# Six of twelve row pairs by seven products in the second feed-forward product, on one core

## The chip, the cores and the metric

The kernel runs on one core of a Trainium2 chip. The metric is the device time of one execution in microseconds. Of the core's engines the text names PE (TensorE: matmuls, with its weight loads as PEld), DVE (VectorE), ACT (ScalarE), POOL (GpSimd) and SP (SyncE, which issues most transfers).

## The reference

A trunk of two layers over 256 tokens of 2048 features, in fp32. Each layer is a token mixer and a feed-forward part, each with a normalization in front and a residual sum behind:

```python
for layer in range(DEPTH):                      # 2
    hn = rms_norm(h, norm_mix[layer])
    mix = mlstm_mixer(hn, ...) if layer % 2 == 0 else rglru_mixer(hn, ...)
    h = h + mix
    h = h + swiglu(rms_norm(h, norm_ffn[layer]), ffn_w_in[layer], ffn_w_out[layer])
return rms_norm(h, norm_final)

def swiglu(x, w_in, w_out):                     # 2048 -> 2 x 5632 -> 2048
    g, u = jnp.split(x @ w_in, 2, axis=-1)
    return (jax.nn.silu(g) * u) @ w_out
```

The change concerns the product with `w_out` in both layers, and some memory that the first normalization and the first mixer use.

## The kernel before

**Numbers in two halves.** A fp32 matrix is split into a high half (a cast to fp32r on ACT, L452) and a low half (what is left, a subtraction on DVE, L453); `split_store` does both. A product is three matmuls: high by high (L390), high by low (L391), low by high (L392). For weights the halves are the tiles `whi` and `wlo`; the loaded weights are `raw`. Low halves come last, so the first matmul that reads a `wlo` (L391) is the one that waits if DVE is late.

**Pairs.** `paired` multiplies two blocks of 128 tokens with two blocks of 512 columns, over row blocks taken two at a time. A plain pair is 2 x 2 x 2 block products, 8 x 3 = 24 matmuls; DVE makes two `wlo` of 1024 columns for it. A pair in the list `seven` is multiplied by a scheme with seven products instead of eight, as Strassen's does: 21 matmuls, but DVE has to form four sums or differences of weight blocks (L403, L404, L405, L407, each 512 columns) and four splits (`s`, `u`, `v`, `t`, of 1024, 512, 1024 and 1024 columns; L401, L402, L406, L408). The third split, `v`, waits for L405. The seven products also need the activations in seven forms instead of four. `raw`, `whi` and `wlo` have six buffers each in the feed-forward layers (four in `wpool`, two in the layer's own pool); a seven-pair uses two of `raw` and four of each of the others, a plain pair two of each.

**A feed-forward layer** (`ffn`). The 5632 hidden columns are taken in two chunks, `CHUNKS`: of 6 and 5 groups of 512 columns. A group (`group`) is the first product for 512 columns of both halves: 8 row pairs, of which `SEVEN_IN` = 2, 4, 6 by seven; the first group of a layer takes the pairs in the order `FIRST`. Its result `e` is turned by `turn` into two row pairs of the hidden matrix, `hid`, with 7 or 4 forms a row pair, according to the list for the second product. This is put off by `later` and runs some steps into the next group. After the groups of a chunk come two calls of `add_out`, each the second product for 1024 of the 2048 output columns over the chunk's 12 or 10 row pairs, of which `SEVEN_OUT` says which go by seven. After the last seven-pair, `sums` and `mid` add the shared banks up and into `h` on DVE (L478 to L482, L778); after the last pair four more sums follow (L789). The very last product takes its pairs in another order, with the two last ones held back.

**Order.** The program is written in order; a scheduler fixes the order of each engine's queue ahead of time, and every engine works its queue in order. `later` and `run_pending` put small pieces of work between the steps of a product: `run_pending` is called once a step with the step's length, and starts the first piece that is due.

**The start.** `par_src` lists the small parameters. Seven transfers on SP bring them in as rows (`rows`, three tiles); `par_cols(i)` transposes one of the three sets on PE and copies it to `cols`. Set 0 holds the first gains and is needed at once. Sets 1 and 2 are transposed after the first product of the first mixer (`linear_wide` ... `"qk00"`, L516 to L518). Between the steps of that product the quarters 1 to 3 of the normalization `n0` are made, each followed by an empty piece:

```python
for q in range(1, 4):
    later(lambda q=q: n0.quarter(q))
    later(lambda: None)
```

`n0.quarter(3)` writes the tile with the tag `x3` of `xpool`. `mask` is a constant of the first mixer, made by POOL and read at L593. `const` is a pool that lives for the whole program; `mx` is the first mixer's and is freed after it.

Of the kernel before, what the change touches and what calls it, by code (L numbers as in the profile page):

```python
# [8 lines left out]
F32 = mybir.dt.float32  # L9
F32R = mybir.dt.float32r  # L10
AF = mybir.ActivationFunctionType
ALU = mybir.AluOpType
PSUM = bass.MemoryType.PSUM

P = 128
# [11 lines left out]
BIG = 1e30  # L27
AHEAD = 1000

SEVEN_IN = (2, 4, 6)  # L30
SEVEN_OUT = {12: (2, 4, 6, 8, 10), 10: (2, 4, 6, 8)}
FIRST = (0, 1, 3, 2, 5, 4, 6, 7)
SEVEN_VO = (3, 5)
CHUNKS = ((0, 6), (6, 11))
# [5 lines left out]
def kernel(  # L40
# [21 lines left out]
    nc = tc.nc  # L62
    const = ctx.enter_context(tc.tile_pool(name="const", bufs=1))
    small = ctx.enter_context(tc.tile_pool(name="small", bufs=2))
    wpool = ctx.enter_context(tc.tile_pool(name="wpool", bufs=4))
    xpool = ctx.enter_context(tc.tile_pool(name="xpool", bufs=1))
# [29 lines left out]
    def load_x():  # L96
        for q in range(4):
            nc.sync.dma_start(h[:, :, q * NB:(q + 1) * NB], xv[:, :, q * NB:(q + 1) * NB])
            if q < 2:
                for kg in (4 * q, 4 * q + 2):  # L100
                    if kg:
                        raw0[kg] = load_raw(m_w_in[0], 0, NB, kg)


    ident = const.tile([P, P], F32, name="ident")
# [7 lines left out]
    for i in range(12):  # L113
        nc.tensor.matmul(pwarm[:, 0:P], lhsT=ones, rhs=ones, start=(i == 0), stop=(i == 11))
    mhalf = const.tile([P, 2], F32, name="mhalf")
    nc.vector.memset(mhalf, -0.5)
    mask = const.tile([P, P], F32, name="mask")
    nc.gpsimd.memset(mask, 0.0)
    nc.gpsimd.affine_select(
        out=mask, in_=mask, compare_op=ALU.is_ge, fill=BIG, base=0,  # L120
        pattern=[[1, P]], channel_multiplier=-1,
    )


    par_src = [
        ("g_mix", norm_mix.rearrange("l (k p) -> (l k) p", p=P), 32),
# [5 lines left out]
        ("cw", r_conv_w.rearrange("l j (k p) -> (l j k) p", p=P), 64),  # L132
    ]
    par = {}
    rows = [const.tile([P, P], F32, name=f"rows{i}") for i in range(3)]
    cols = [const.tile([P, P], F32, name=f"cols{i}") for i in range(3)]
    part, at, used = 0, 0, [0, 0, 0]
    for name, src, n in par_src:
        if part == 0 and at or at + n > P:
            part, at = part + 1, 0  # L140
        nc.sync.dma_start(rows[part][at:at + n, :], src)
        if part == 0:
            load_x()
        par[name] = cols[part][:, at:at + n]
        at += n
        used[part] = at
# [3 lines left out]
    def par_cols(i):  # L150
        n = used[i]
        pt = misc(f"par{i}")
        nc.tensor.transpose(pt[:, 0:n], rows[i][0:n, :], ident[0:n, 0:n])
        with tc.high_priority(offset=AHEAD):
            return nc.vector.tensor_copy(cols[i][:, 0:n], pt[:, 0:n])

    gains = par_cols(0)


# [4 lines left out]
    def later(fn, after=0.0):  # L164
        pending.append((work[0] + after, fn))
# [60 lines left out]
    def linear_wide(w, c0, nk, act, act2, name, soon=2):  # L226

        ps = [acc(f"{name}_{f}") for f in range(4)]
        for k, hi, lo in stream(w, c0, nk):
            for f0 in (0, 2):  # L230
                for f in (f0, f0 + 1):
                    nc.tensor.matmul(ps[f], lhsT=hi[:, f * P:(f + 1) * P], rhs=act2(k), start=(k == 0), stop=False,  # L232
                                     skip_group_check=True)
                for f in (f0, f0 + 1):
                    nc.tensor.matmul(ps[f][:, 0:T], lhsT=lo[:, f * P:(f + 1) * P], rhs=act(k)[0], start=False,  # L235
                                     stop=(k == nk - 1), skip_group_check=True)
            run_pending(1.39, k >= soon)
        return ps
# [6 lines left out]
    def bc4(ap):  # L245
        return ap.unsqueeze(1).broadcast_to([P, 4, T])
# [226 lines left out]
    part = {}  # L473
# [19 lines left out]
    for i in range(6):  # L493
        nc.tensor.matmul(idle[:, 0:P], lhsT=ident, rhs=h[:, 0, 0:P], start=(i == 0), stop=(i == 5))
    for q in range(1, 4):
        later(lambda q=q: n0.quarter(q))
        later(lambda: None)
    n1 = Pairs("f0", par["g_ffn"][:, 0:16])

    def mlstm_mixer():  # L500
        with tc.tile_pool(name="mx", bufs=2) as mx:
            w = m_w_in[0]
            scratch["pool"] = mx
            ys = [[mx.tile([P, 4, T], F32R, tag=f"y{s}{j}", name=f"y{s}{j}", bufs=1) for s in "hl"] for j in range(4)]
            scratch["get"] = lambda: mx.tile([P, NT * 2 * (DV + 1)], F32, tag="vs", name="zt")[:, 0:4 * T]
            sel = mx.tile([H, H, P], F32R, tag="y", name="sel", bufs=1)
# [7 lines left out]
            gsel = mx.tile([4 * H, 2 * H], F32, name="gsel", bufs=1)  # L514
            nc.gpsimd.tensor_tensor(gsel, ident[0:4 * H, 0:2 * H], ident[0:4 * H, 2 * H:4 * H], op=ALU.add)
            ps_q0 = linear_wide(w, 0, NK, n0.act, n0.act2, "qk00", soon=0)  # L516
            par_cols(1)
            par_cols(2)  # L518
            with tc.issue_after(n0.last.ins):
                for q in range(4):  # L520
                    n0.stats(q)
# [115 lines left out]
            for half in range(2):  # L637
                for which, dst, sc in ((0, qT, 1.0), (1, kT, DK ** -0.5)):
                    ps = ps_q0
                    if half or which:  # L640
# [4 lines left out]
                        out=d4, in0=d4, scalar=sc, in1=bc4(n0.bc), op0=ALU.mult, op1=ALU.mult,  # L645
# [82 lines left out]
            project_out(m_w_out[0], NK, lambda k: (yh[k // 4][:, k % 4, :], yl[k // 4][:, k % 4, :]), n1)  # L728

    mlstm_mixer()  # L730


    def ffn(layer, n, nxt):
        with tc.tile_pool(name=f"ff{layer}", bufs=1) as fp:
# [56 lines left out]
            for c0, c1 in CHUNKS:  # L791
                np_ = 2 * (c1 - c0)
                seven = SEVEN_OUT[np_]
                hid = [
# [221 lines left out]
```

## Time and profile before

| | us |
|---|---|
| median of 3 runs | 2095.54 (2095.53 to 2095.84) |
| the profiled execution | 2092.44 |
| its span, first to last instruction | 2090.5 |
| PE busy | 2075.5 (99%) |
| PE weight loads busy | 1732.5 (83%) |
| DVE busy | 1838.1 (88%) |
| ACT busy | 1200.3 (57%) |
| granted clock of PE | 0.999 of full speed |

Times in the profile are from the start of the span. A row of the order of time has start, duration, engine, line, operation, output and inputs, the shape, the count, and in brackets the idle time of the engine before it with what ended it. A row of the waits has who waited for whom, microseconds in total, times, the longest. A row of the windows has the stretch, its length, and for PE, PEld, DVE, ACT and POOL the busy time with the number of instructions, then the granted clock, the share of the transfer engines and GB/s. The first layer's groups start at 394 us and its feed-forward part ends at about 1090; the second layer's goes from 1384 to the end.

### The profile page before, as it was taken

Reading aid. Unit: us, or ns where it says so; the run is one execution under the profiler, and the core shown is the slowest. Engines: PE = TensorE matmul, PEld = TensorE weight load, DVE = VectorE, ACT = ScalarE, POOL = GpSimd, SP = SyncE. Lnnn points to the kernel's source line nnn. Section 1 sums busy time; section 2 is a strip of 40 time slices with the busy share of each in tenths; the row PEclk is TensorE's granted clock in tenths of the full one; section 3 lists DMA queues with packets and bytes.
Section 4 is the critical chain, followed back from the end, with each engine's and each line's share of the span. In section 5 each row is a group of like instructions: output and inputs, shape, how many; then the busy total and the mean of one; then the engine's idle time right before and its main releaser. Section 6 shows DMA issues by size and latency. Waiting matters only on the chain.

```text
span 2090.5 us, 27102 instructions
## 1 busy us (share of the span) xinstructions
PE 2075.5 (99%) x9770; PEld 1732.5 (83%) x9770; DVE 1838.1 (88%) x2362; ACT 1200.3 (57%) x1553; POOL 26.1 (1%) x44
## 2 busy tenths in 40 slices
PE   9999999999999999999999999999999999999997
PEld 7888888888888888888888888888888888888886
DVE  7678886799999999999997888679999999999998
ACT  6446555565555555555656778556555555555554
POOL 0000000000000000000000000000000000000010
PEclk9999999999999999999999999999999999999999
DMA  7556655656565665665656666666655666656564
GB/s 217 172 171 190 182 181 177 204 188 228 173 200 202 201 201 201 202 218 185 202 186 177 191 183 191 191 192 208 206 193 185 201 207 202 205 198 220 191 202 141
DMA packets 211374, 405.71 MB, mean 194 GB/s; under 512 B 14552, under 2 KB 14760, under 8 KB 211112
## 3 DMA queue, kind: packets, MB, share of 16 engines
q1 hardware_dynamic: 210520, 401.89, 59.7%
q10 hardware_dynamic: 720, 2.10, 0.3%
q8 instruction: 76, 1.25, 0.2%
q14 instruction: 58, 0.48, 0.1%
HBM read 401.84 MB, written 2.10 MB: 193 GB/s over the span
## 4 chain that ended last, share of the span: by engine, by line
PE 94%; DVE 3%; issue 1%; ACT 1%; DMA 1%; POOL 0%; POOLq 0%; SPq 0%; ACTq 0%; DVEq 0%
PE p L392 15%; PE p L391 15%; PE p L390 15%; PE po L391 7%; PE po L392 7%; PE po L390 7%; PE rec L232 3%; PE gb L232 3%; PE po L208 3%; PE po L206 3%; PE po L207 3%; PE vo L390 2%; PE vo L392 2%; PE vo L391 2%; PE qk L232 2%; PE gb L235 1%
## 5 line engine op out<-in xcount | busy, mean ns | idle before, releaser
L452 ACT CAST whi<-raw 128x1024 fp32r<-128x1024 f32 (+1 forms) x812 | 768.3, 992 | 652.6 <-DVE raw L405 354.7
L453 DVE TENSOR_TENSOR wlo<-raw,whi 128x1024 fp32r<-128x1024 f32 (+1 forms) x812 | 897.4, 1149 | 94.8 <-ACT whi L452 90.5
L390 PE MATMUL p<-whi,z_f 128*128 128x512 f32 x1342 | 523.8, 390 | 0.0
L392 PE MATMUL p<-whi,z_f 128*128 128x512 f32 x1342 | 522.2, 389 | 0.0
L391 PE MATMUL p<-wlo,z_f 128*128 128x512 f32 x1342 | 522.2, 389 | 0.0
L392 PEld LDWEIGHTS p<-whi,z_f 128*128 128x128 f32 x1342 | 251.9, 188 | 52.3
L391 PEld LDWEIGHTS p<-wlo,z_f 128*128 128x128 f32 x1342 | 252.0, 188 | 51.6
L390 PEld LDWEIGHTS p<-whi,z_f 128*128 128x128 f32 x1342 | 252.0, 188 | 51.6
L178 DVE TENSOR_TENSOR wlo<-raw,whi 128x1024 fp32r<-128x1024 f32 (+1 forms) x161 | 195.2, 1215 | 87.7 <-ACT whi L176 87.5
L391 PE MATMUL po<-wlo,h 128*128 128x512 f32 x668 | 260.6, 390 | 1.7 <-DVE wlo L453 1.7
L392 PE MATMUL po<-whi,h 128*128 128x512 f32 x668 | 260.0, 389 | 0.0
L390 PE MATMUL po<-whi,h 128*128 128x512 f32 x668 | 259.3, 390 | 0.0
L176 ACT CAST whi<-raw 128x1024 fp32r<-128x1024 f32 (+1 forms) x161 | 168.0, 1046 | 130.7 <-PE po L208 58.7
L391 PEld LDWEIGHTS po<-wlo,h 128*128 128x128 f32 x668 | 125.4, 188 | 29.4 <-DVE wlo L453 3.5
L392 PEld LDWEIGHTS po<-whi,h 128*128 128x128 f32 x668 | 125.4, 188 | 25.9
L390 PEld LDWEIGHTS po<-whi,h 128*128 128x128 f32 x668 | 125.3, 188 | 25.9 <-ACT whi L452 0.2
L390 PE MATMUL vo<-whi,x_m 128*128 128x512 f32 x240 | 95.8, 399 | 0.5 <-DVE yl L697 0.5
L392 PE MATMUL vo<-whi,x_m 128*128 128x512 f32 x240 | 93.5, 390 | 0.0
L391 PE MATMUL vo<-wlo,x_m 128*128 128x512 f32 x240 | 93.5, 390 | 0.0
L232 PE MATMUL qk<-x_m,whi 128*128 128x512 f32 x256 | 81.1, 399 | 0.0
L232 PE MATMUL rec<-x_m,whi 128*128 128x512 f32 x256 | 80.6, 396 | 0.0
L232 PE MATMUL gb<-x_m,whi 128*128 128x512 f32 x256 | 80.4, 395 | 0.0
(272 smaller groups left out, 2431.6 us busy)
## 6 DMA issues: line engine op xcount, KB each, us to landing
raw<-in_ffn_w_in_dram SPq DMA_DIRECT2D x352, 512.0 KB, 4.9
raw<-in_ffn_w_out_dram SPq DMA_DIRECT2D x176, 512.0 KB, 5.4
raw<-in_m_w_in_dram SPq DMA_DIRECT2D x95, 512.0 KB, 4.0
raw<-in_r_w_in_dram SPq DMA_DIRECT2D x64, 512.0 KB, 3.9
raw<-in_m_w_out_dram SPq DMA_DIRECT2D x32, 512.0 KB, 3.9
raw<-in_r_w_out_dram SPq DMA_DIRECT2D x32, 512.0 KB, 3.9
gr<-in_r_gate_w_dram SPq DMA_DIRECT2D x8, 512.0 KB, 3.6
h<-in_x_dram SPq DMA_DIRECT2D x4, 512.0 KB, 8.2
```

Source lines behind the costliest of these rows:

```text
L176: cast = nc.scalar.copy(hi[:, at, 0:ncols], r)
L178: nc.vector.tensor_tensor(lo[:, at, 0:ncols], r, hi[:, at, 0:ncols].bitcast(F32), op=ALU.subtract)
L206: nc.tensor.matmul(o, lhsT=ah[:, bs], rhs=hi, start=(k == 0), stop=False)
L207: nc.tensor.matmul(o, lhsT=ah[:, bs], rhs=lo, start=False, stop=False)
L208: nc.tensor.matmul(o, lhsT=al[:, bs], rhs=hi, start=False, stop=(k == nk - 1))
L232: nc.tensor.matmul(ps[f], lhsT=hi[:, f * P:(f + 1) * P], rhs=act2(k), start=(k == 0), stop=False, skip_group_check=True)
L235: nc.tensor.matmul(ps[f][:, 0:T], lhsT=lo[:, f * P:(f + 1) * P], rhs=act(k)[0], start=False, stop=(k == nk - 1), skip_group_check=True)
L390: nc.tensor.matmul(o, lhsT=ah, rhs=bh, start=i not in begun, stop=False)
L391: nc.tensor.matmul(o, lhsT=ah, rhs=bl, start=False, stop=False)
L392: nc.tensor.matmul(o, lhsT=al, rhs=bh, start=False, stop=stop and p == end[i])
L452: nc.scalar.copy(dst_hi, src)
L453: nc.vector.tensor_tensor(dst_lo, src, dst_hi.bitcast(F32), op=ALU.subtract)
```

## The change

In `SEVEN_OUT` the 12-pair products get six pairs by seven instead of five, at other places, and the 10-pair products keep four, at other places. Neighbouring pairs (4 and 5, 7 and 8) are then both by seven. Row pairs 5 and 7 are stored in seven forms and row pair 6 in four, so one tile grows more than before. The rows of the parameters move from `const` into one tile with the tag `x3` of `xpool`, which quarter 3 of `n0` overwrites; for that, `par_cols(1)` and `par_cols(2)` move ahead of quarter 3, into the steps of the first product, in place of two empty pieces. `mask` moves from `const` to `mx` and is made there.

```diff
-SEVEN_OUT = {12: (2, 4, 6, 8, 10), 10: (2, 4, 6, 8)}
+SEVEN_OUT = {12: (2, 4, 5, 7, 8, 10), 10: (2, 4, 5, 8)}
...
-    mask = const.tile([P, P], F32, name="mask")
-    nc.gpsimd.memset(mask, 0.0)
-    nc.gpsimd.affine_select(
-        out=mask, in_=mask, compare_op=ALU.is_ge, fill=BIG, base=0,
-        pattern=[[1, P]], channel_multiplier=-1,
-    )
...
-    rows = [const.tile([P, P], F32, name=f"rows{i}") for i in range(3)]
+    rows = xpool.tile([P, 3, P], F32, tag="x3", name="rows")
...
-        nc.sync.dma_start(rows[part][at:at + n, :], src)
+        nc.sync.dma_start(rows[at:at + n, part, :], src)
...
-        nc.tensor.transpose(pt[:, 0:n], rows[i][0:n, :], ident[0:n, 0:n])
+        nc.tensor.transpose(pt[:, 0:n], rows[0:n, i, :], ident[0:n, 0:n])
...
     for q in range(1, 4):
+        if q == 3:
+            for i in (1, 2):
+                later(lambda i=i: par_cols(i))
         later(lambda q=q: n0.quarter(q))
-        later(lambda: None)
+        if q < 2:
+            later(lambda: None)
...
+            mask = mx.tile([P, P], F32, name="mask", bufs=1)
+            nc.gpsimd.memset(mask, 0.0)
+            nc.gpsimd.affine_select(
+                out=mask, in_=mask, compare_op=ALU.is_ge, fill=BIG, base=0,
+                pattern=[[1, P]], channel_multiplier=-1,
+            )
...
             ps_q0 = linear_wide(w, 0, NK, n0.act, n0.act2, "qk00", soon=0)
-            par_cols(1)
-            par_cols(2)
```

## The prediction

> **What bounds the kernel now.** I read the page first, then the waits of the matrix engine (PE), then the share of each engine in the two products that change, and last the order of time on the vector engine (DVE) there.
>
> ```profile
> PE 2075.5 (99%) x9770; PEld 1732.5 (83%) x9770; DVE 1838.1 (88%) x2362; ACT 1200.3 (57%) x1553; POOL 26.1 (1%) x44
> PE po L391 <- DVE wlo L453: 1.7, 2, 0.9
> 649.47:711.37 61.90, 61.90 (x278) 51.35 (x278) 57.95 (x68) 33.58 (x39) 0.00 (x0) 1.00 0.60 198
> 711.37:773.20 61.83, 61.83 (x274) 51.22 (x273) 57.40 (x65) 32.29 (x35) 0.00 (x0) 1.00 0.63 207
> 489.95 0.87 PE th L746 x8
> 532.32 0.87 PE th L746 x8
> ```
>
> PE is never idle in the two feed-forward layers except near the end; the second row, from the waits, is the longest entry: 1.7 us in two waits, both in the last product. So the time is the sum of PE's work. But the windows, which are the two 12-pair products of the first layer, show DVE (the fourth column of times, 57.95 of 61.90) nearly full as well. PE's own pace comes from the chain of waits: one group, 183 matmuls and 8 transposes, lasts 532.32 - 489.95 = 42.37, so a matmul costs (42.37 - 0.87) / 183 = 0.2268 us. A plain pair (24 matmuls) is 5.44, a pair by seven products (21) is 4.76.
>
> The question is whether DVE can feed PE faster. Its pace in a 12-pair product:
>
> ```profile
> 669.23 1.23 DVE L453 TENSOR_TENSOR wlo<-raw,whi 128x1024 fp32r<-128x1024 f32 x1 [0.45 <-ACT whi L452]
> 675.51 0.68 DVE L403 TENSOR_TENSOR raw<-raw,raw 128x512 f32<-128x512 f32 x1
> 685.13 0.69 DVE L403 TENSOR_TENSOR raw<-raw,raw 128x512 f32<-128x512 f32 x1
> 698.54 3.50 DVE L453 TENSOR_TENSOR wlo<-raw,whi 128x1024 fp32r<-128x1024 f32 x3 [0.47 <-ACT whi L452]
> 702.29 1.23 DVE L453 TENSOR_TENSOR wlo<-raw,whi 128x1024 fp32r<-128x1024 f32 x1 [0.26 <-ACT whi L452]
> 703.73 1.23 DVE L453 TENSOR_TENSOR wlo<-raw,whi 128x1024 fp32r<-128x1024 f32 x1 [0.21 <-ACT whi L452]
> 720.61 1.23 DVE L453 TENSOR_TENSOR wlo<-raw,whi 128x1024 fp32r<-128x1024 f32 x1 [0.68 <-ACT whi L452]
> 672.63 0.39 PE L391 MATMUL po<-wlo,h 128*128 128x512 f32 x1
> 703.23 0.39 PE L391 MATMUL po<-wlo,h 128*128 128x512 f32 x1
> 724.31 0.39 PE L391 MATMUL po<-wlo,h 128*128 128x512 f32 x1
> ```
>
> From L403 of one seven-pair to L403 of the next, with one plain pair between, DVE takes 685.13 - 675.51 = 9.62, PE 4.76 + 5.44 = 10.20: DVE gains 0.58 for every such two. The kernel has one place in each layer where two seven-pairs already stand next to each other, the first group (order 0, 1, 3, 2, 5, 4, 6, 7):
>
> ```profile
> 419.54 1.22 DVE L453 TENSOR_TENSOR wlo<-raw,whi 128x1024 fp32r<-128x1024 f32 x1 [0.46 <-ACT whi L452]
> 426.89 1.22 DVE L453 TENSOR_TENSOR wlo<-raw,whi 128x1024 fp32r<-128x1024 f32 x1 [0.47 <-ACT whi L452]
> 423.79 0.39 PE L391 MATMUL p<-wlo,z_f 128*128 128x512 f32 x1
> 428.55 0.39 PE L391 MATMUL p<-wlo,z_f 128*128 128x512 f32 x1
> 2065.28 1.22 DVE L453 TENSOR_TENSOR wlo<-raw,whi 128x1024 fp32r<-128x1024 f32 x1 [0.47 <-ACT whi L452]
> 2066.56 0.50 PE L391 MATMUL po<-wlo,h 128*128 128x512 f32 x1
> 2071.70 0.50 PE L391 MATMUL po<-wlo,h 128*128 128x512 f32 x1 [0.74 <-DVE wlo L453]
> ```
>
> These are the third split (code L406) of pairs 4 and 6: DVE needs 426.89 - 419.54 = 7.35 for a seven-pair, PE consumes it in 428.55 - 423.79 = 4.76. **Each pair of neighbours costs DVE 2.59 us of its lead.** A plain pair is 9.62 - 7.35 = 2.27 on DVE.
>
> The lead itself: I define the **reserve** as the time from DVE's start of a third split to PE's first L391 on it, less 1.28. That is 2066.56 - 2065.28, in the last product, where PE has just caught up with DVE (its matmul slipped about 0.1). At reserve zero PE waits. At pair 4 of the first product it is 672.63 - 669.23 - 1.28 = 2.12; at pair 10, 703.23 - 698.54 - 1.28 = 3.41; at pair 2 of the second product, 724.31 - 720.61 - 1.28 = 2.42.
>
> **The change, part by part.** *Matmuls.* The 12-pair product has six seven-pairs instead of five, so PE loses 3 x 0.2268 = 0.68 in each of four products (two per layer, two layers): -2.72 us. The 10-pair products keep four.
>
> *DVE in the 12-pair products.* The seven-pairs become 2, 4, 5, 7, 8, 10: neighbours at 4-5 and 7-8, one plain pair between 2-4, 5-7, 8-10. I carry the reserve along, +0.58 over a plain pair, -2.59 over neighbours, and where it falls below zero PE waits and it restarts at zero.
> First product: 2.12 at pair 4; pair 5: -0.47, a wait of 0.47; pair 7: 0.58; pair 8: -2.01, a wait of 2.01; pair 10: 0.58.
> On to pair 2 of the second: DVE takes 720.61 - 698.54 = 22.07, of which 0.26 + 0.21 and 0.68 - 0.47 are waits for room (0.47 is a seven-pair's own wait for ScalarE), so 21.39; PE takes 724.31 - 703.23 = 21.08. The reserve is 0.58 - 0.31 = 0.27 instead of 2.42.
> Second product: pair 4: 0.85; pair 5: -1.74, wait 1.74; pair 7: 0.58; pair 8: wait 2.01.
> Sum 6.23 a layer, 12.46 for both, as layer 1 starts from the same reserve:
>
> ```profile
> 1659.07 1.23 DVE L453 TENSOR_TENSOR wlo<-raw,whi 128x1024 fp32r<-128x1024 f32 x1 [0.45 <-ACT whi L452]
> 1662.48 0.39 PE L391 MATMUL po<-wlo,h 128*128 128x512 f32 x1
> 1004.56 1.23 DVE L453 TENSOR_TENSOR wlo<-raw,whi 128x1024 fp32r<-128x1024 f32 x1 [0.16 <-ACT whi L452]
> 1008.26 0.39 PE L391 MATMUL po<-wlo,h 128*128 128x512 f32 x1
> 1994.89 1.22 DVE L453 TENSOR_TENSOR wlo<-raw,whi 128x1024 fp32r<-128x1024 f32 x1
> 1998.31 0.39 PE L391 MATMUL po<-wlo,h 128*128 128x512 f32 x1
> ```
>
> (1662.48 - 1659.07 - 1.28 = 2.13.) The waits are the balance of a deficit, so they cannot be had back elsewhere in the product: what hid DVE's work before was the reserve, and it is spent.
>
> *DVE in the 10-pair products.* Seven-pairs 2, 4, 5, 8. Reserve at pair 4: 1008.26 - 1004.56 - 1.28 = 2.42, so pair 5 waits 0.17; I take the same for the second one. In layer 1, 1998.31 - 1994.89 - 1.28 = 2.14: 0.45. Two plain pairs follow and refill it. The very last product has the same DVE work as before, and PE waits for DVE at its end already (0.74 at 2071.70), so a wait at pair 5 there is taken off that one: 0. Sum 0.8, bounds 0 and 2.
>
> *The hidden rows.* One more row pair per layer is stored in seven forms (line 752).
>
> ```profile
> 661.75 0.28 DVE L332 SCALAR_TENSOR_TENSOR zh<-zh 128x128 f32<-128x128 f32 x1
> 664.30 1.09 DVE L453 TENSOR_TENSOR h<-zh,h 128x896 fp32r<-128x896 f32 x1
> 17.38 0.40 PE L232 MATMUL qk<-x_m,whi 128*128 128x512 f32 x1
> 35.00 0.26 PE L153 MATMUL par<-ident,rows 112*128 112x112 f32 x1
> 36.62 0.67 PE L321 MATMUL bc_m<-dg_m,ones 128*128 128x256 f32 x2 [1.15 <-DVE dg_m L319]
> 12.87 0.55 SPq L141 DMA_DIRECT2D rows<-in_r_conv_w_dram  x1
> DMA to landing us min/median/max: 2.3/6.2/8.2
> L593 DVE SCALAR_TENSOR_TENSOR pe<-mb,ucol,mask x16: 340/344/351, 71.1 to 156.6; 128x128 f32<-128x128 f32 x16
> ```
>
> That is four short subtractions and 896 instead of 512 columns: at most 4 x 0.28 + 1.09 = 2.2 on DVE. It falls into the group after the one that makes pairs 4 and 5, three groups ahead of the product; the reserve covers it there, and three groups refill it. 0; if it does not refill, up to 2.2 a layer goes onto pair 5's wait.
>
> *Rows and mask.* The rows' seven transfers keep their place on SyncE's queue. Two transposes (0.26 each at most) and two copies leave the place at 35.00, just ahead of PE's 1.15 wait, where they cost nothing, and go behind the fourth and fifth step of the first product, about 17.3 and 18.8; the normalization's last quarter moves one step (1.39) later, and is used only at step 12. The last transfer is issued at 12.87; by the fastest landing that is 15.2, by the slowest 21.1. PE would wait 0 to 3.8 for it, with everything behind it. I take 0: 6.2 and 8.2 belong to transfers queued behind the big ones for x and the first weights. PE's 0.5 moved into the stream is returned by the shorter wait at 36.62. One tile for all three row sets could tie the first transpose to the last transfer, but h is one tile with four loads, and PE begins on its first quarter; so no. The mask is first read at 71.1, and POOL has nothing between 2.8 and 35.2; 0. Start-up: 0, bounds -0.3 and +3.8.
>
> **Sum.** -2.72 + 12.46 + 0.8 = +10.5. The profiled execution took 2092.44 (span 2090.5), so 2102.9; the median of the runs, 2095.54, lies 3.1 above it, so 2106.0.
>
> [...]
>
> **The rivals.**
> *The reserve holds: no slower.* The mechanism is that DVE needs only its busy time, the 0.47 gaps being filled by the next pair's splits. Point of decision: a seven-pair at 6.8 or less, so that two products need 2 x (57.95 + 6.8 - 2.27 - 61.22) = 2.5 more than PE gives, about the reserve of 2.12. Result -2.72 + 2 x 0.4, so 2093.6; with no wait at all 2092.8. [...] For it: 88% on the page. Against it: the neighbours at 419.54 keep their gap of 0.47.
> *The reserve refills between the products*, because the products' sums are placed otherwise: pair 2 of the second stands at 2.42 again, pair 4 at 3.00, pair 5 at 0.41 without a wait, pair 7 at 0.99, and pair 8 waits 1.60: 1.60 instead of 3.75, twice 2.15 less, 2101.7. Against it: 21.39 over 21.08.
> *Worse:* each wait costs a restart (the slip of 0.1 at 2066.56, ten times 1), the extra forms eat the reserve of pair 5 (up to 4.4), or the start waits for the rows (3.8): 2108 to 2112.
>
> **How the numbers follow.** The forecast has 0.62, the refill 0.13, the holding reserve 0.17, worse 0.08. A change under 0.2% (4.2 us, so 2091.3 to 2099.7) is not told from none: the holding reserve lies there, its full saving of 2.72 being under 4.2; only with a gain at the start (0.02 to 0.03) would it be faster. So faster 0.03, same 0.15, slower 0.82. The likeliest case alone runs from 2102 to 2111; down to 2096 it takes in the refill and half-covered waits, up to 2111.5 most of the worse cases.
>
> **What would show it.** In the 12-pair products, waits of PE at L391 for DVE's wlo, near 2 us at pair 8 and 0.5 and 1.7 at pair 5, none at pair 10; DVE without waits for room there, and its time per neighbour 7.35; PE's weight loads in those windows below 83%. The four products have 12 matmuls fewer; no new wait ahead of 36 us. I am wrong if the neighbours run faster than 7.35, or if PE's waits there stay under 1 us in all.

## The result, and the profile after

The changed kernel is slower: its median is 2107.40 us (2105.14 to 2109.06), beside 2094.99 us (2092.46 to 2095.84) of the kernel before in the same comparison. The ratio is 1.0065, 95% interval 1.0054 to 1.0075. The profiled execution took 2107.24 us with a span of 2105.4 us, 14.9 us longer than the span before. Most line numbers that matter are lower by 7 now: L391 is L384, L453 is L446, L403 is L396, L321 is L314; the sums into `h` are L779 and L790.

The page of the changed kernel, first the busy time of each engine, then the share of the span that each engine has in the chain that ended last:

```profile
PE 2083.4 (99%) x9758; PEld 1728.2 (82%) x9758; DVE 1852.6 (88%) x2394; ACT 1205.1 (57%) x1565; POOL 24.7 (1%) x44
PE 86%; DVE 8%; issue 2%; DMA 2%; ACT 2%; POOL 0%; ACTq 0%; POOLq 0%; SPq 0%; DVEq 0%
```

PE has the 12 matmuls less that were forecast (9758 for 9770) and yet 7.9 us more busy time. DVE has 32 operations and 14.5 us more. The chain runs over DVE for 8% of the span. The waits of PE in the changed kernel say where:

```profile
PE po L384 <- DVE wlo L446: 5.2, 8, 1.4
PE bc_m L314 <- DVE dg_m L312: 3.5, 1, 3.5
PE tr_m L273 <- DVE h L790: 0.9, 1, 0.9
PE po L383 <- ACT whi L445: 0.8, 2, 0.6
```

The first row is the wait that was forecast, the second product (`po`) waiting for low halves. The second is one wait of 3.5 us in the start, where 1.15 us stood before. The third is new: the normalization behind the first layer waits for the last sum into `h`.

To place the 14.9 us I cut both spans at the first matmul of each stage and compare the lengths of the stretches. As an example, this is the window between the cuts around the two 12-pair products of the first layer, in the kernel before:

```profile
648.39:773.05 124.66, 124.66 (x556) 103.34 (x554) 116.28 (x134) 66.81 (x75) 0.00 (x0) 1.00 0.62 204
```

And in the changed kernel:

```profile
653.40:781.34 127.94, 125.93 (x550) 100.97 (x548) 120.45 (x143) 68.24 (x78) 0.00 (x0) 1.00 0.59 190
```

127.94 for 124.66 is +3.3. The other stretches, cut in the same way, in us against the profile before (the groups of both chunks of a layer are taken together; "10-pair + mixer" reaches from the first 10-pair product to the second layer's first group; "last" is the second layer's 10-pair products):

| kernel | start | groups L0 | 12-pair L0 | 10-pair + mixer | groups L1 | 12-pair L1 | last | span |
|---|---|---|---|---|---|---|---|---|
| after | +4.7 | +1.0 | +3.3 | +2.6 | +0.9 | +2.3 | +0.2 | +14.9 |
| start_only | +3.8 | 0 | 0 | 0 | 0 | 0 | +0.4 | +4.1 |
| quarter_back | -0.1 | +1.0 | +3.4 | +2.4 | +0.9 | +2.8 | +1.1 | +11.4 |
| gp_first | -1.0 | +0.9 | +4.7 | +2.0 | +1.3 | +2.3 | +0.5 | +10.6 |
| less_dve | +2.1 | +0.7 | -1.4 | +0.2 | +0.6 | -1.4 | -1.9 | -1.0 |
| ten_only | +4.4 | +0.3 | 0 | +0.6 | +0.3 | 0 | +0.3 | +5.9 |
| half_casts | +5.4 | +0.6 | +1.8 | +0.6 | +0.8 | +1.3 | -0.9 | +9.5 |
| six_spread | +3.4 | +0.6 | +3.8 | +0.1 | +0.7 | +2.5 | +0.3 | +11.5 |
| best2 | -1.2 | 0 | +5.6 | +0.1 | 0 | +4.3 | -0.9 | +7.9 |
| best1 | -1.6 | +0.6 | +1.9 | +0.4 | +0.8 | +2.0 | -0.7 | +3.4 |
| before_two | -1.5 | 0 | 0 | 0 | +0.4 | 0 | -0.6 | -1.8 |

Each row is one profiled execution; a row is read with some tenths of a microsecond of doubt: in start_only the stretches that no edit touches agree within 0.02, but the last one differs by 0.4. The starts of the kernels that share the changed start differ by more, 2.1 to 5.4, and with them PE's wait and its granted clock; the last section has the numbers.

**The start.** The order of time of the changed kernel, ACT and PE:

```profile
16.84 0.26 PE L146 MATMUL par<-ident,rows 112*128 112x112 f32 x1
20.16 1.03 PE L273 MATMUL tr_m<-ident,h 128*128 128x128 f32 x8
26.98 0.62 ACT L255 ACTIVATE junk<-h 128x512 bf16<-128x512 f32 x1
38.68 1.22 PE L314 MATMUL bc_m<-dg_m,ones 128*128 128x256 f32 x2 [3.54 <-DVE dg_m L312]
39.34 6.34 PE L526 MATMUL gp<-x_m,gwx 128*32 128x512 f32 x16
```

And the rows of the kernel before that answer to the second, the third and the last:

```profile
18.78 1.03 PE L280 MATMUL tr_m<-ident,h 128*128 128x128 f32 x8
25.79 0.63 ACT L262 ACTIVATE junk<-h 128x512 bf16<-128x512 f32 x1
36.94 4.05 PE L525 MATMUL gp<-x_m,gwx 128*32 128x512 f32 x16
```

PE takes the moved rows at 16.84 without a wait, and quarter 3 a step later (20.16 for 18.78). `junk` is the sum of squares of the normalization; the program orders it behind the last ACT operation of quarter 3 (L520; L519 in the kernel before). With quarter 3 a step later, the first square starts 1.19 later (26.98 for 25.79), and the matrix `bc_m` that its result leads to comes 2.06 later (38.68 for 36.62). PE's wait grows from 1.15 to 3.54, and the 16 `gp` matmuls behind it start 2.4 later (39.34 for 36.94). Then they take 6.34 for 4.05, another 2.3. Together that is the +4.7. The second half is the clock (the third number from the end). First two windows of the changed kernel, then one of the kernel before:

```profile
38.00:44.00 6.00, 5.32 (x13) 2.42 (x14) 4.28 (x12) 0.37 (x1) 0.11 (x1) 0.50 0.61 175
44.00:46.00 2.00, 2.00 (x10) 1.15 (x9) 0.00 (x0) 0.29 (x2) 0.00 (x0) 0.93 0.00 0
```

```profile
38.00:44.00 6.00, 6.00 (x31) 4.14 (x30) 5.83 (x20) 1.85 (x7) 0.21 (x2) 1.00 0.63 178
```

From 38.68 on PE waits for nothing there and gets half its clock until about 44 us; before, it had its full clock.

### The profile page after: what moved, and what is told of

It is laid out like the page before. It is cut to its first block, busy times and chain, and to the rows that moved or that the text cites. A ratio compares the mean times of both kernels' runs of the same rounds, so it can differ in the third digit from the quotient of the medians.

```text
span 2105.4 us, 27093 instructions
## 1 busy us (share of the span) xinstructions
PE 2083.4 (99%) x9758; PEld 1728.2 (82%) x9758; DVE 1852.6 (88%) x2394; ACT 1205.1 (57%) x1565; POOL 24.7 (1%) x44
## 4 chain that ended last, share of the span: by engine, by line
PE 86%; DVE 8%; issue 2%; DMA 2%; ACT 2%; POOL 0%; ACTq 0%; POOLq 0%; SPq 0%; DVEq 0%
PE p L383 15%; PE p L384 14%; PE p L385 14%; DVE wlo L446 4%; PE po L384 4%; PE po L385 4%; PE po L383 4%; PE gb L225 3%; PE po L201 3%; PE po L199 3%; PE po L200 3%; PE rec L225 3%; PE qk L225 2%; PE vo L383 2%; PE vo L385 2%; PE vo L384 2%
## 5 line engine op out<-in xcount | busy, mean ns | idle before, releaser
L446 DVE TENSOR_TENSOR wlo<-raw,whi 128x1024 fp32r<-128x1024 f32 (+1 forms) x820 | 905.2, 1148 | 92.7 <-ACT whi L445 89.8
L384 PE MATMUL p<-wlo,z_f 128*128 128x512 f32 x1342 | 522.4, 389 | 0.0
L383 PE MATMUL p<-whi,z_f 128*128 128x512 f32 x1342 | 520.2, 391 | 0.0
L383 PEld LDWEIGHTS p<-whi,z_f 128*128 128x128 f32 x1342 | 251.8, 188 | 53.4 <-ACT zh L752 1.7
L384 PEld LDWEIGHTS p<-wlo,z_f 128*128 128x128 f32 x1342 | 252.0, 188 | 52.3 <-DVE wlo L446 0.8
L384 PE MATMUL po<-wlo,h 128*128 128x512 f32 x664 | 259.3, 392 | 5.3 <-DVE wlo L446 5.2
L385 PE MATMUL po<-whi,h 128*128 128x512 f32 x664 | 258.1, 390 | 0.0
L383 PE MATMUL po<-whi,h 128*128 128x512 f32 x664 | 254.2, 393 | 0.8 <-ACT whi L445 0.8
L384 PEld LDWEIGHTS po<-wlo,h 128*128 128x128 f32 x664 | 124.6, 188 | 37.0 <-DVE wlo L446 11.1
L383 PEld LDWEIGHTS po<-whi,h 128*128 128x128 f32 x664 | 123.5, 188 | 30.6 <-ACT whi L445 5.9
L383 PE MATMUL vo<-whi,x_m 128*128 128x512 f32 x240 | 95.8, 399 | 0.5 <-DVE yl L698 0.5
L384 PE MATMUL vo<-wlo,x_m 128*128 128x512 f32 x240 | 93.5, 390 | 0.0
L398 DVE TENSOR_TENSOR raw<-raw,raw 128x512 f32<-128x512 f32 x114 | 78.8, 691 | 3.3
L400 DVE TENSOR_TENSOR raw<-raw,raw 128x512 f32<-128x512 f32 x114 | 78.8, 691 | 3.3
L397 DVE TENSOR_TENSOR raw<-raw 128x512 f32<-128x512 f32 x114 | 78.7, 690 | 3.3
```

The lines of the kernel that those rows point to most:

```text
L383: nc.tensor.matmul(o, lhsT=ah, rhs=bh, start=i not in begun, stop=False)
L384: nc.tensor.matmul(o, lhsT=ah, rhs=bl, start=False, stop=False)
L385: nc.tensor.matmul(o, lhsT=al, rhs=bh, start=False, stop=stop and p == end[i])
L397: nc.vector.tensor_tensor(rb[:, 0, :], rb[:, 1, :], rb[:, 0, :], op=ALU.subtract)
L398: nc.vector.tensor_tensor(rb[:, 1, :], rb[:, 1, :], ra[:, 0, :], op=ALU.add)
L400: nc.vector.tensor_tensor(ra[:, 1, :], ra[:, 1, :], rb[:, 1, :], op=ALU.subtract)
```

## The experiments

**start_only: rows, mask and order of the start alone.**

```diff
-SEVEN_OUT = {12: (2, 4, 5, 7, 8, 10), 10: (2, 4, 5, 8)}
+SEVEN_OUT = {12: (2, 4, 6, 8, 10), 10: (2, 4, 6, 8)}
```

> The changed kernel with the old places of the pairs by seven: only rows, mask and the order of the start are changed. Theory (the trace of the changed kernel: the products lose some 11 us, the start 4.7): PE's wait ahead of the broadcast at about 38 us is 3.5, the granted clock falls to 0.5 behind it, and the whole is 4.7 us above the kernel before, about 2099.7. Rival (my prediction: the start costs nothing, and the 4.7 is an accident of one execution): within 1 us of the kernel before, 2095.

Measured: 2096.65 beside 2092.99, ratio 1.0018 (1.0008 to 1.0027). The profile has +3.8 of its +4.1 in the start and nothing else above 0.4. Its wait of PE in the start:

```profile
PE bc_m L314 <- DVE dg_m L312: 3.4, 1, 3.4
```

That is 3.7 us above the kernel before, less than the 4.7 expected: the slow clock was shorter in this kernel (0.72 over 38 to 44 us, 0.50 in the changed kernel). So between a quarter and a third of the loss has nothing to do with the pairs.

**quarter_back: quarter 3 back in its old step**, with both transposes in the one step ahead of it.

```diff
-            for i in (1, 2):
-                later(lambda i=i: par_cols(i))
+            later(lambda: [par_cols(i) for i in (1, 2)])
```

> The changed kernel with both late transposes in one piece, so that quarter 3 of the normalization is issued at the step where it was before. Theory A (the squares for the sums are issued behind quarter 3, so the chain to the broadcast is late because quarter 3 is): the wait at about 37 us returns to about 1.2, the clock stays at 1.0, 4 to 4.7 us below the changed kernel, about 2103. Theory B (the small work on the recurrent layer's parameter, now ready early and placed among the chain on DVE, makes it late): the wait stays near 3.5 and the time within 1 us of 2107.

Measured: 2104.39, ratio 1.0054 (1.0039 to 1.0069), which is 3.0 below the changed kernel and less than the 4 to 4.7 expected; the start is at -0.1. The +1.1 of its last stretch holds a fall of the clock near the end, which the last section shows. The order of time of this kernel, ACT and PE, and its window from 38 to 44 us:

```profile
25.67 0.64 ACT L255 ACTIVATE junk<-h 128x512 bf16<-128x512 f32 x1
36.56 0.67 PE L314 MATMUL bc_m<-dg_m,ones 128*128 128x256 f32 x2 [1.23 <-DVE spa_p L462]
36.88 4.05 PE L525 MATMUL gp<-x_m,gwx 128*32 128x512 f32 x16
```

```profile
38.00:44.00 6.00, 6.00 (x31) 4.18 (x30) 5.48 (x18) 1.43 (x5) 0.21 (x2) 1.00 0.61 176
```

Square, wait, clock and `gp` are all back. The two transposes are still in the first product, the rows are still in `x3`, the mask is still in `mx`: these cost nothing that the profile shows. The place of quarter 3 is the cause of the whole loss at the start. Why 1.19 at the square becomes 2.06 at `bc_m` I did not follow up.

**gp_first: the 16 `gp` matmuls ahead of the normalization's end.**

```diff
-            n0.finish()
             for ...:            # the 16 gp matmuls
...
+            n0.finish()
```

> The changed kernel with the 16 gate matmuls ahead of the end of the normalization, so that PE has 3.7 us of work where it waits now. Theory (a wait of 3.5 on a chain that is not PE's, and a halved clock behind it): no wait over 0.5 us, clock 1.0 throughout, 5 to 6 us below the changed kernel, about 2101.5. Rival (the clock falls for another reason than the idle time): the wait of 3.5 goes, but the clock falls all the same, and 3 us or less is gained.

Measured: 2101.36, ratio 1.0039 (1.0024 to 1.0054). Quarter 3 is as late as in the changed kernel, but the matmuls that were queued behind the waiting `bc_m` now stand ahead of it (PE's order of time in this kernel, and the same window):

```profile
35.35 3.87 PE L525 MATMUL gp<-x_m,gwx 128*32 128x512 f32 x16
39.36 0.67 PE L314 MATMUL bc_m<-dg_m,ones 128*128 128x256 f32 x2
```

```profile
38.00:44.00 6.00, 5.86 (x32) 4.43 (x30) 5.36 (x17) 2.73 (x7) 0.80 (x2) 1.00 0.65 177
```

There is no wait left, the clock stays at 1.00, and the start is 1.0 shorter than before. The lateness itself cost nothing as soon as PE had something else to do.

**less_dve: one of the four differences of a seven-pair not made** in the second product only. The kernel multiplies with the unchanged block in its place.

```diff
-                nc.vector.tensor_tensor(rb[:, 0, :], rb[:, 1, :], rb[:, 0, :], op=ALU.subtract)
+                if name[:2] != "po":
+                    nc.vector.tensor_tensor(rb[:, 0, :], rb[:, 1, :], rb[:, 0, :], op=ALU.subtract)
```

> The changed kernel without one of the four differences of weights (the second, 0.69 us on DVE) in the pairs by seven of the second product alone; the values of those products are then others than the reference's. PE has the same matmuls. Theory (PE waits in those products because DVE has more work than PE): 4.3 us less DVE work in a 12-pair product turns the deficit of about 1 to 4 into a surplus; the waits of 1.2 to 2.8 a product go, those of the 10-pair products too: 8 to 10 us below the changed kernel, 2097 to 2099. Rival (buffers or the order of the queues make PE wait, not the amount of work): under 2 us gained.

Measured: 2093.11 beside 2092.99, ratio 1.0000 (0.9991 to 1.0010), although the start still loses 2.1 in its profile. This is 14.3 below the changed kernel, where 8 to 10 were expected. The window of the two 12-pair products, and the longest wait of PE in the second products of the whole program:

```profile
650.80:774.10 123.30, 123.30 (x550) 102.19 (x549) 115.71 (x134) 69.13 (x79) 0.00 (x0) 1.00 0.62 206
```

```profile
PE po L384 <- DVE wlo L447: 0.4, 1, 0.4
```

PE does not idle at all in this window, and it is 1.36 shorter than before (124.66): that is 2 x 0.68, the whole saving of six matmuls. The matmuls' part of the sum was right, and 0.7 us of DVE work in each seven-pair is enough to turn it into a loss.

**ten_only: new places in the 10-pair products alone** (the start as changed).

```diff
-SEVEN_OUT = {12: (2, 4, 5, 7, 8, 10), 10: (2, 4, 5, 8)}
+SEVEN_OUT = {12: (2, 4, 6, 8, 10), 10: (2, 4, 5, 8)}
```

> The changed kernel with the old places in the 12-pair products and the new ones (2, 4, 5, 8) in the 10-pair products: as many matmuls as before, as much DVE work, two neighbours. Theory A (a run of neighbours spends the reserve even where the total is enough): PE waits at pair 5, the first layer's 10-pair products with the recurrent layer behind them take 2 to 2.6 us longer than before as in the changed kernel, and the kernel is 2 to 3 above start_only, 2099. Theory B (only the total counts, and what was seen there is an after-effect of the 12-pair products): within 1 us of start_only, 2096.7.

Measured: 2098.19 beside 2093.24, ratio 1.0022 (1.0013 to 1.0031). Neither expectation holds as it was put: the 10-pair products with the mixer lose 0.6 in the first layer, not 2 to 2.6, and the last stretch 0.3, but the kernel is 1.5 above start_only, more than the 1 of theory B. The groups lose 0.3 in each layer, and the start 4.4 for 3.8.

**half_casts: the seven-pair's gap closed.** The cast of the third split is made in two halves, so that ACT has done one when DVE comes from L398.

```diff
                 nc.vector.tensor_tensor(rb[:, 0, :], rb[:, 1, :], rb[:, 0, :], op=ALU.subtract)
+                nc.scalar.copy(vh[:, 0, :], rb[:, 0, :])
                 nc.vector.tensor_tensor(...)    # L398
-                split_store(vh, vl, rb)
+                nc.scalar.copy(vh[:, 1, :], rb[:, 1, :])
+                nc.vector.tensor_tensor(vl, rb, vh.bitcast(F32), op=ALU.subtract)
```

> The changed kernel with the third cast of a pair by seven made in two halves on ACT, the first as soon as its half of the weights is there, so that DVE need not sit idle for it. Theory (what the products lose is the amount of DVE time, gaps included): 0.4 us less for most pairs by seven, 2 to 4 us of the waits in each layer's 12-pair products gone, and 1 to 2 us at the 10-pair products, together 4 to 9 us below the changed kernel. Rival (the queues are ordered such that the gaps are filled already, or ACT's extra instruction is late): under 1.5 us gained.

Measured: 2101.94, ratio 1.0046 (1.0030 to 1.0062). Window of the 12-pair products, and the starts of pairs 7 and 8 in DVE's order of time:

```profile
654.10:780.60 126.50, 125.37 (x550) 101.39 (x549) 122.57 (x145) 71.47 (x91) 0.00 (x0) 1.00 0.60 197
```

```profile
687.95 0.68 DVE L396 TENSOR_TENSOR raw<-raw,raw 128x512 f32<-128x512 f32 x1
694.75 0.69 DVE L396 TENSOR_TENSOR raw<-raw,raw 128x512 f32<-128x512 f32 x1
```

A neighbour takes DVE 694.75 - 687.95 = 6.80 now. The 12-pair products lose 1.8 and 1.3 instead of 3.3 and 2.3, and 10-pair products and mixer 0.6 instead of 2.6. The whole is 5.5 below the changed kernel, within the 4 to 9 expected, but the 12-pair products gained 1.5 and 1.0 where 2 to 4 each were expected.

**six_spread: six pairs by seven, but only one couple of neighbours, at the front** (1 and 2), and the 10-pair products as before. The hidden rows' turn is due earlier, as pair 1 needs it.

```diff
-SEVEN_OUT = {12: (2, 4, 5, 7, 8, 10), 10: (2, 4, 5, 8)}
+SEVEN_OUT = {12: (1, 2, 4, 6, 8, 10), 10: (2, 4, 6, 8)}
...
-                later(lambda: [turn(j, i, hid, (ea, eb)) for i in range(2)], 8.0)
+                later(lambda: [turn(j, i, hid, (ea, eb)) for i in range(2)], 5.0)
```

> The changed kernel with six pairs by seven of 12 at 1, 2, 4, 6, 8, 10 (one pair of neighbours, where the reserve is largest) and the old places in the 10-pair products; the turned rows are due 5 instead of 8 us after their group, so that they come between the first two steps. PE and DVE have the changed kernel's work in the 12-pair products. Theory A (the amount of work decides): the 12-pair products lose 2 to 4 us a layer against the kernel before, as in the changed kernel; the 10-pair products nothing; 2 to 3 below the changed kernel in all. Theory B (the neighbours decide): the 12-pair products take 1.4 us less than before in each layer; 8 to 9 below the changed kernel, 2098 to 2099.

Measured: 2105.25, ratio 1.0058 (1.0044 to 1.0072). The 12-pair products lose 3.8 and 2.5, no less than with two couples of neighbours. So it is not the number of neighbours as such: the sixth pair's work did not fit in either placement. The loss need not be the same one, though: PE's waits in the second products are 2.8 us for low halves (`po` at L384) and 1.9 for high halves (L383) here, 5.2 and 0.8 in the changed kernel, and the earlier turn is a second edit that no run takes apart.

**best2: quarter_back, gp_first, half_casts and six_spread together.**

```diff
-SEVEN_OUT = {12: (2, 4, 5, 7, 8, 10), 10: (2, 4, 5, 8)}
+SEVEN_OUT = {12: (1, 2, 4, 6, 8, 10), 10: (2, 4, 6, 8)}     # and turn due at 5.0
...
+            later(lambda: [par_cols(i) for i in (1, 2)])        # ahead of quarter 3
+            n0.finish()                                         # behind the gp matmuls
+                nc.scalar.copy(vh[:, 0, :], rb[:, 0, :])        # and vh[:, 1, :] behind L398
```

> All four edits on the changed kernel: quarter 3 back at its step, the gate matmuls ahead of the end of the normalization, the third cast in halves, and the places of six_spread. Theory (deficit of DVE, plus the start): the start 1 us faster than before, the 12-pair products within 1 us of 1.4 faster than before, the 10-pair products as before: 2 to 4 us below the kernel before, 2090. Rival (the deficit stays over 2 us a layer): within 1 us of the kernel before or slower.

Measured: 2100.17, ratio 1.0031 (1.0020 to 1.0043). The start is at -1.2 as it should be, but the 12-pair products lose 5.6 and 4.3, more than with six_spread or half_casts alone. Here my theory that the gains add up fell. PE waits 2.1 us for ACT's high halves there, but 1.9 in six_spread too, which has no halved casts; why the two together lose more than either stays open.

**best1: the same with the places of the change.**

```diff
 SEVEN_OUT = {12: (2, 4, 5, 7, 8, 10), 10: (2, 4, 5, 8)}        # turn due at 8.0
...
+            later(lambda: [par_cols(i) for i in (1, 2)])
+            n0.finish()                                         # behind the gp matmuls
+                nc.scalar.copy(vh[:, 0, :], rb[:, 0, :])        # and vh[:, 1, :] behind L398
```

> The changed kernel, places as changed, with three edits: quarter 3 back at its step, the gate matmuls ahead of the end of the normalization, the third cast in halves. Theory (the sections add up: the start as in gp_first, the products as in half_casts): start -1, 12-pair products +1.9 and +1.3, 10-pair products +0.6, groups +1.2, end -0.9 against the kernel before: 3 above it, 2096. Rival (the queues' order makes a product lose up to 2 more when anything ahead of it is changed, as in best2): 6 or more above.

Measured: 2096.34 beside 2093.31, ratio 1.0012 (1.0003 to 1.0021). With both helps at the start and the gap closed, the 12-pair products still lose 1.9 and 2.0.

**before_two: the kernel before, with gp_first and half_casts.** Five pairs by seven at the old places, rows and mask in `const`.

```diff
 SEVEN_OUT = {12: (2, 4, 6, 8, 10), 10: (2, 4, 6, 8)}
...
+            n0.finish()                                         # behind the gp matmuls
+                nc.scalar.copy(vh[:, 0, :], rb[:, 0, :])        # and vh[:, 1, :] behind L405
```

> The kernel before with two edits alone: the gate matmuls ahead of the end of the normalization, and the third cast in halves. No change of the pairs by seven. Theory (PE's two places of idle time in the kernel before are the wait of 1.2 at 36 us and those of the last product, 1.7): the start 1.1 faster, the last section about 0.9 faster as in best2, 1.5 to 2.5 below the kernel before, ratio 0.9990. Rival (the order of the queues shifts elsewhere, as in the 12-pair products of best2): no faster than before.

Measured: 2090.55 beside 2093.31, ratio 0.9988 (0.9979 to 0.9997), the only kernel of these that is faster than the one before. The longest waits of PE in it:

```profile
PE tr_m L280 <- DMA h<-in_x_dram: 1.5, 1, 1.5
PE po L391 <- DVE wlo L408: 1.4, 1, 1.4
```

The wait at `bc_m` is not among them: the start is 1.5 shorter, the last products 0.6. It keeps nothing of the change.

## Why the prediction was right, and where only in sum

**The forecast against the stretches.** The sum was +10.5 against the profiled execution, and that execution of the changed kernel is 14.8 longer (2107.24 for 2092.44). That the median forecast, 2106.0, came within 1.4 of 2107.4 is luck in two ways. The profiled execution before lies 3.1 below the median that I started from, and the one after lies at its median. And the errors of the terms offset each other: the 12-pair products were forecast at 12.46 - 2.72 = +9.7 and cost 3.3 + 2.3 = +5.6; everything else was forecast at +0.8 and cost +9.3. The direction and the range held, and so did the main mechanism, that DVE cannot do the sixth pair's work in time; the places and sizes of the waits and three other terms did not.

**The matmuls: right.** 12 less, and 0.68 a product, as less_dve shows.

**DVE as the bound of the 12-pair products: right in kind, too large.** With six matmuls less the window should have become 1.36 shorter and became 3.3 longer, so the waits came to 4.7 in the first layer, and in the second to 1.36 + 2.3 = 3.7, where 6.23 each were forecast. Only 2.01 of the 4.7 is idle time in the window (127.94 - 125.93); the other 2.7 is in PE's busy time, which rose with six matmuls less: 125.93 / 550 = 0.2290 a matmul for 124.66 / 556 = 0.2242. In less_dve, where PE has the same matmuls and DVE less work, it is 123.30 / 550 = 0.2242 again; so these 2.7 go back to DVE's work too, in matmuls that are shown as longer ones. Not all of it is waiting for DVE's low halves: added up over the matmuls that start late, 2.5 us of the loss stand at L384, which reads a low half, and 1.5 at L383, which reads a high half from ACT.

My test, waits "near 2 us at pair 8 and 0.5 and 1.7 at pair 5, none at pair 10", failed. Only the 0.5 at pair 5 of the first product is there, as matmuls that start late at 682.8. Around pair 8, which DVE begins at 694.69, no matmul starts more than about 0.1 late. The longest wait of the window is one of 1.31, and it belongs to pair 10, which DVE begins at 703.57. Its row, and what it waited for on DVE and on ACT; then ACT's row of the waits in this window, and the one of the kernel before:

```profile
710.41 0.50 PE L384 MATMUL po<-wlo,h 128*128 128x512 f32 x1 [1.31 <-DVE wlo L446]
707.39 1.22 DVE L446 TENSOR_TENSOR wlo<-raw,whi 128x1024 fp32r<-128x1024 f32 x1 [1.68 <-ACT whi L445]
706.31 4.04 ACT L445 CAST whi<-raw 128x1024 fp32r<-128x1024 f32 x4 [4.18 <-DMA raw<-in_ffn_w_out_dram]
ACT whi L445 <- DMA raw<-in_ffn_w_out_dram: 16.7, 5, 5.4
ACT whi L452 <- DMA raw<-in_ffn_w_out_dram: 0.5, 1, 0.5
```

DVE was not at work in front of this wait: it sat idle for ACT, and ACT for weights that were still on their way. Such a transfer is issued when a split of DVE frees one of the six buffers of `raw` (this one at 700.74; 45 of the 49 waits ahead of SP's issues in this window, 99.9 us, end with such a split), and in this window it takes 3.5 to 6.3 us to land. So a late DVE also makes its own weights late, a term that my sum does not have. In less_dve ACT waits 0.3 for these transfers. What part of the loss would go with more buffers, or with transfers issued earlier, no run shows.

The term that was mis-sized is "+0.58 over a plain pair". DVE's order of time of the changed kernel, at each seven-pair's first difference; the first five rows are pairs 4, 5, 7, 8, 10 of the first product, the other five those of the second:

```profile
670.91 0.68 DVE L396 TENSOR_TENSOR raw<-raw,raw 128x512 f32<-128x512 f32 x1
678.25 0.69 DVE L396 TENSOR_TENSOR raw<-raw,raw 128x512 f32<-128x512 f32 x1
687.26 0.69 DVE L396 TENSOR_TENSOR raw<-raw,raw 128x512 f32<-128x512 f32 x1
694.69 0.69 DVE L396 TENSOR_TENSOR raw<-raw,raw 128x512 f32<-128x512 f32 x1
703.57 0.69 DVE L396 TENSOR_TENSOR raw<-raw,raw 128x512 f32<-128x512 f32 x1
...
735.49 0.68 DVE L396 TENSOR_TENSOR raw<-raw,raw 128x512 f32<-128x512 f32 x1
742.83 0.69 DVE L396 TENSOR_TENSOR raw<-raw,raw 128x512 f32<-128x512 f32 x1
751.72 0.69 DVE L396 TENSOR_TENSOR raw<-raw,raw 128x512 f32<-128x512 f32 x1
759.65 0.68 DVE L396 TENSOR_TENSOR raw<-raw,raw 128x512 f32<-128x512 f32 x1
769.07 0.68 DVE L396 TENSOR_TENSOR raw<-raw,raw 128x512 f32<-128x512 f32 x1
```

The first neighbours take 678.25 - 670.91 = 7.34 and 742.83 - 735.49 = 7.34, the predicted 7.35; the second ones 7.43 and 7.93. But a seven-pair with the plain pair behind it takes 9.01, 8.88, 8.89 and 9.42, not 9.62. From pair 4 to pair 10 that is 32.66 and 33.58, where twice 7.35 + 9.62 are 33.94: 1.6 less for the two products, about what the forecast was too high by (6.2 - 4.7 = 1.5). That these two agree so well is partly luck, as the wait at pair 10 is not in this balance. The reason for the shorter stretches stands in the rows inside such a pair:

```profile
679.69 0.69 DVE L398 TENSOR_TENSOR raw<-raw,raw 128x512 f32<-128x512 f32 x1
680.30 2.43 DVE L446 TENSOR_TENSOR wlo<-raw,whi 128x1024 fp32r<-128x1024 f32 x2
682.65 0.68 DVE L400 TENSOR_TENSOR raw<-raw,raw 128x512 f32<-128x512 f32 x1
683.25 4.09 DVE L446 TENSOR_TENSOR wlo<-raw,whi 128x1024 fp32r<-128x1024 f32 x4
...
690.67 4.09 DVE L446 TENSOR_TENSOR wlo<-raw,whi 128x1024 fp32r<-128x1024 f32 x4 [0.55 <-ACT whi L445]
```

Six splits stand between the first difference of pair 5 and that of pair 7: two of pair 5, two of the plain pair, and the first two of pair 7. Two of the six stand between L398 and L400, and four follow without a gap. At pair 7, whose neighbour is pair 8, all four splits stand behind L400, after a gap of 0.55. In a new order of pairs the scheduler laid DVE's queue in another way, and the splits filled the 0.47 that I had taken as belonging to a pair. This is the mechanism of the rival "the reserve holds", which I had dismissed with the neighbours at 419.54: neighbours do keep their gap, pairs next to a plain one need not. It came true in part, and half_casts shows what the rest is worth. The new order has its price too: the split at 707.39 was laid between L398 and L400 of pair 10 in the same way, and there it was the one that waited for its weights. DVE's share of busy time did not show room here: with DVE at 120.45 of 127.94, 94%, PE was already waiting for it.

**The 10-pair products: mis-sized.** Forecast 0.8 for both layers, measured 2.6 (with the mixer) and 0.2. In the first layer 0.9 of it is the wait at `tr_m` for the last sum into `h`, a place for which I had no step. ten_only, with these places, loses 0.6, six_spread, with a late DVE in the 12-pair products, 0.1; only both together lose 2 and more (after, quarter_back, gp_first), and with the gap closed it is 0.6. So the products were wrongly costed one by one; how the one hands its lateness to the other I have not shown.

**The hidden rows and refill: 0 forecast**, bound 2.2 a layer; the groups lose 1.0 and 0.9. Of this, 0.3 falls in each chunk on its fourth group, in which row pairs 4 and 5 are now both brought into seven forms, one behind the other; in ten_only, with the old 12-pair places, this is the whole loss, 0.3 in the second chunk of each layer. So "the reserve covers it there" was wrong by 0.3 a chunk. The rest, 0.3 to 0.4 a layer, falls in the first two groups behind the 12-pair products, and I did not follow it up.

**The start: the step that failed.** I wrote that the last quarter "is used only at step 12", and set the start at 0 with "no new wait ahead of 36 us". I had looked for the reader of the quarter's result, and not for what is queued behind its instructions: the squares wait for its last ACT operation. The two transposes, the landing of the rows and the tile of `x3`, of which I had spoken at length, cost nothing (quarter_back). A fall of the clock was not in the sum at all.

## What to carry to other kernels

When a piece of work is moved to a later step, ask first what is ordered behind it on its own engine, not who reads its result (here the square came 1.19 us later, and `bc_m` 2.06); and where a wait cannot be shortened, put ready matmuls ahead of it (gp_first: no wait where 3.54 us stood, and a start 1.0 shorter than before instead of 4.7 longer). Before the change PE was never idle in the first layer's two 12-pair products and DVE, which feeds it, was busy for 116.28 of 124.66 us, 93%, and the trade from one to the other found little room: a saving of 0.68 us of PE for some 5 us of DVE (7.35 - 2.27) was a loss from the moment the reserve was spent, 3.3 and 2.3 us in the 12-pair products of the two layers. Ask also what the feeding engine frees: with DVE late, the transfers that wait for its buffers were late too (ACT waited 16.7 us for them in these products, 0.5 before). A duration that holds a gap is not a constant of its pair (9.01 for 9.62 where the gap was filled), and waits below some tenths of a microsecond are read from the time per matmul, not from the list of waits (0.2290 for 0.2242, 2.7 of the 4.7 us).

## What the runs showed of the hardware

In the changed kernel, in which PE is 99% busy, a single idle time of 3.5 us ended at a granted clock of 0.50, and the fall cost as much as the idle time that was added (2.3 and 2.4 us). PE's wait ahead of `bc_m` and the granted clock from 38 to 44 us were: 1.2 and 1.00 (before, quarter_back), 1.7 and 1.00 (less_dve), 3.1 and 0.50 (ten_only), 3.1 and 0.72 (six_spread), 3.4 and 0.72 (start_only), 3.5 and 0.50 (after), 3.8 and 0.53 (half_casts), no wait and 1.00 (gp_first, best2, before_two); best1 has no such wait either, and a mean clock of 0.999. The same wait of 3.1 thus stands before two different clocks. The slow time was not of one length either: in start_only the clock was 0.96 from 38 to 40 us, 0.50 to 42 and 0.85 to 46, in the changed kernel 0.50 from 38 to 44 and 0.93 to 46.

Nor does the length of the wait alone tell in these runs whether the clock falls. In less_dve the clock fell earlier, behind PE's wait of 1.8 for the input `h`, which ends at 7.5 us:

```profile
PE tr_m L273 <- DMA h<-in_x_dram: 1.8, 1, 1.8
8.00:11.00 3.00, 3.00 (x17) 3.00 (x15) 1.66 (x4) 2.53 (x7) 0.00 (x0) 0.50 1.06 411
```

In the kernel before and in the changed kernel that wait is 1.0 and 0.4 us, and the clock of the same window 1.00. PE came later to `bc_m` in less_dve, at 37.1 instead of 35.1, and so waited only 1.7 there, while `bc_m` was as late as in the changed kernel (38.73 and 38.68). In the last product, PE waits 0.6 and 1.4 us one shortly behind the other in quarter_back, in gp_first and in the changed kernel. The window behind these waits, of quarter_back and of gp_first:

```profile
2068.00:2071.00 3.00, 3.00 (x9) 2.32 (x8) 3.00 (x4) 1.06 (x2) 0.00 (x0) 0.51 0.93 279
2068.00:2071.00 3.00, 2.73 (x12) 2.29 (x13) 3.00 (x4) 1.66 (x3) 0.00 (x0) 1.00 0.79 218
```

The lowest clock in these windows is 0.50, and the same waits end at half clock in one kernel and at full clock in another. A wait of 3.1 us went with a fall (0.50 in ten_only), but so did one of 1.8 in less_dve (0.50), while the 1.7 in front of `bc_m` in that kernel did not (1.00). What decides it, no run shows.
